# Pinning the instruction order across the seam of two output projections, and squaring a row in its own buffer

## The chip, the cores and the metric

The kernel runs on one core of a Trainium2 chip. The metric is device time in microseconds (us) of one execution. In the text PE is the matrix engine (TensorE), DVE is VectorE, ACT is ScalarE, POOL is GpSimd and SP is SyncE; POOL and SP mostly issue DMAs here.

## The reference

One transformer-like layer over a sequence of 1024 positions with width 1024, in float32. What matters here is the end of its first sub-layer and the start of the second:

```python
merged = sigmoid(gate_a) * a_out + sigmoid(gate_b) * b_out   # (1024, 1024)
x  = x + gt1 * (merged @ w_o)                                # output projection, residual
h2 = rmsnorm(x, norm2_g) * (1.0 + sc2) + sh2                 # needs sum(x*x) over the width
f_gate, f_up = split(h2 @ w_ffn_in)                          # 2 x 2816 wide
x  = x + gt2 * ((silu(f_gate) * f_up) @ w_ffn_out)
```

The root-mean-square norm needs, for each position, the sum of the squares of all 1024 values of the new `x`. So no row of `h2` can be made before the last block of the output projection is finished.

## The kernel before

**Layout.** Everything is kept transposed: 128 channels on the partitions, positions along the free dimension. The sequence is worked in two halves of 512 positions (`hf` 0 and 1). The output projection is a loop over `hf` and, inside it, over eight blocks `d` of 128 output channels (line 1330 and after). Each product is made of float32r matmuls in three passes: both operands are split in a high part and a rest, and `mm3` issues high x high, high x low, low x high. One block `d` is 8 x 3 = 24 matmuls into one PSUM bank; four such banks (`mm`) rotate.

**What one block d does.** I write d0 to d7 for the blocks of half 0 and d0' to d7' for those of half 1.

- `unit(w_o[d+1])` prepares the next weight block, one step ahead: SP loads it into one of three `raw` buffers, ACT copies it to a high part `wh`, DVE subtracts for the rest `wl`. Each of `wh` and `wl` has three buffers.
- `store(xk, x_rows(hf, d))`, despite its name a load issued on POOL's queue, brings 128x512 of the residual `x` into `xk`, one of two buffers of the tag `xs`.
- after the 24 matmuls, DVE forms the new row block `x1` from the bank, the gate `gt1` and `xk` (one scalar_tensor_tensor, called STT below). In half 0, `x1` lies in a `tmp()` buffer: tag `t2`, shown as `t` in the profile, four buffers.
- `sumsq` squares `x1` on ACT, for d > 0 into another `tmp()` buffer, and DVE adds it to the running sum `ss`. For d = 0 the square goes straight to `ss`. There is one `ss` buffer, so half 1's cannot be written before half 0's has been read.
- `store(x1d, x1)` writes the row block to DRAM, again on POOL's queue.
- in half 0 only: `m_split(m1, d-1)` splits a row of half 1's merged input (ACT cast, DVE subtraction), `m_load(m1, 1, d)` loads the next such row into one of two `hs` buffers, and for d = 1 to 6 `ada_next` does one 128x1024 dot product of the adaLN modulation on DVE (`mid<-mid,silu_c`, then a small `mod<-acc_mod,cc`). d7 splits both of the last two rows, 6 and 7; row 7 is loaded right before, when row 5's split has freed a buffer.
- in half 1 only: at d1', before its matmuls, `col_rstd(sums[0])` turns `ss` of half 0 into column sums with eight small matmuls (`at<-ones,ss`), DVE scales them (`ms`), POOL takes the power -1/2 (`rcol`), and before the matmuls of d2' `spread` broadcasts it over a bank (`at<-ident,rcol`). From then on `mod2` normalises half 0's rows. At d2' and d4', `first_unit` loads and splits the 128x1024 weight blocks `w_gate[4]` and `w_gate[5]` ahead of time into long-lived buffers (`j<-raw`).

**What sets the order.** A planner orders each engine's instructions at build time, by its own cost model and by which inputs it takes to be ready; program order is only a priority. The engines then run that order strictly. While the flag `in_order[0]` is true, each instruction issued through the wrapper is pinned behind the instruction traced just before it on the same engine:

```python
def call(*args, **kw):
    ins = f(*args, **kw)              # line 76, the line of nearly all instructions
    if in_order[0]:
        tc.keep_in_program_order(ins)
    return ins
```

This holds for PE, DVE, ACT and POOL arithmetic. DMAs issued on SP by `load` are always pinned; DMAs issued on POOL by `store` never are. In the projection loop the flag is set once in each pass by `in_order[0] = hf == 1 and d > 5` (line 1356), behind the line that issues `unit(w_o[d+1])`, so the weight preparation of a pass still runs under the flag of the pass before.

Of the kernel before, what the change touches and what calls it, by code (L numbers as in the profile page):

```python
# [38 lines left out]
def kernel(  # L39
# [24 lines left out]
    in_order = [False]  # L64
# [35 lines left out]
    def nm(s):  # L100
        n_names[0] += 1
        return f"{s}_{n_names[0]}"

    def mm_bank():
        return psum.tile([P, 512], F32, tag="mm", name=nm("mm"))
# [4 lines left out]
    def tmp(dt=F32):  # L110
        return t2.tile([P, 512], dt, tag="t2", name=nm("t2"))

    def stream(tag):
        return t2.tile([P, 512], F32, tag=tag, name=nm(tag), bufs=2)

    def midt(dt, shape):
        return mid.tile([P, 2048], dt, tag="mid", name=nm("mid")).rearrange(
            "p (a b) -> p a b", a=shape
        )

    def hid():
        return hpool.tile([P, 2048], F32R, tag="h", name=nm("h")).rearrange(
            "p (a b) -> p a b", a=4
        )
# [3 lines left out]
    def jt(dt, shape):  # L128
        return jpools[0].tile([P, 2048], dt, tag="j", name=nm("j")).rearrange(
            "p (a b) -> p a b", a=shape  # L130
        )
# [4 lines left out]
    def load(dst, src):  # L136
        tc.keep_in_program_order(nc.sync.dma_start(dst, src))

    def store(dst, src):
        nc.gpsimd.dma_start(dst, src)  # L140
# [10 lines left out]
    def raw_unit(src):  # L151
        r = wpool.tile([P, UNIT], F32, tag="raw", name=nm("raw"))
        load(r, src)
        return r

    def unit(src, eng=None, raw=None):
        r = raw if raw is not None else raw_unit(src)
        h = wpool.tile([P, UNIT], F32R, tag="wh", name=nm("wh"))
        l = wpool.tile([P, UNIT], F32R, tag="wl", name=nm("wl"))
        A.copy(h, r)  # L160
        (eng or V).tensor_tensor(l, r, h.bitcast(F32), op=ALU.subtract)
        return h, l

    def mm3(out, a, b, first, last):
        T.matmul(out, a[0], b[0], start=first, stop=False)
        T.matmul(out, a[0], b[1], start=False, stop=False)
        T.matmul(out, a[1], b[0], start=False, stop=last)
# [120 lines left out]
    def col_rstd(ss, n, r):  # L288

        pt = at_bank()  # L290
        for i in range(n):
            T.matmul(pt[:, i : i + 1], ss[:, i * P : (i + 1) * P], ones[:, 0:1], start=True, stop=True)
        rstd(pt[:, :n], n, r)

    def spread(r, n):

        bc = at_bank()
        for i in range(n):
            T.matmul(bc[:, i * P : (i + 1) * P], r[:, i : i + 1].to_broadcast([P, P]), ident,
                     start=True, stop=True)  # L300
        return bc[:, : n * P]

    def ss_tile():
        return small.tile([P, 640], F32, tag="ss", name=nm("ss"), bufs=1)

    rcol = [const.tile([P, 5], F32, tag=f"rcol{i}", name=f"rcol{i}") for i in range(4)]

    def sumsq(src, first, ss):
        if first:
            A.activation(ss, src, AF.Square)  # L310
        else:
            q = tmp()
            A.activation(q, src, AF.Square)
            V.tensor_tensor(ss, ss, q, op=ALU.add)

    def modulate(src, rb, k, sc, sh, hH, hL, dst):

        shift = mod[:, sh + k : sh + k + 1]
        V.scalar_tensor_tensor(out=dst, in0=src, scalar=mod[:, sc + k : sc + k + 1], in1=rb,
                               op0=ALU.mult, op1=ALU.mult)  # L320
        A.activation(hH, dst, AF.Identity, bias=shift)
        V.scalar_tensor_tensor(out=hL, in0=dst, scalar=shift, in1=hH.bitcast(F32),
                               op0=ALU.add, op1=ALU.subtract)
# [162 lines left out]
    def first_unit(i):  # L486

        r = raw_unit(w_gate[EARLY - 2 + i])
        h, l = (firsts[p][:, i * UNIT : (i + 1) * UNIT] for p in range(2))
        A.copy(h, r)  # L490
        V.tensor_tensor(l, r, h.bitcast(F32), op=ALU.subtract)
        return h, l
# [22 lines left out]
    def ada_next(more=True):  # L515
        if not ada_ahead:
            return
        col, gain, r = ada_ahead.pop(0)
        ada_dot(r, col)
        ada_end(col, gain)  # L520
        if more:
            ada_load()
# [11 lines left out]
    def ada_pair_load():  # L534
        i = ada_queue[0][0] - GT1
        t = midt(F32, 2)
        store(t, w_ada2[i : i + 2].rearrange("a p b -> p a b"))
        for j in range(2):
            col, gain = ada_queue.pop(0)
            ada_ahead.append((col, gain, t[:, j, :]))  # L540
# [15 lines left out]
    def x_rows(hf, k):  # L556
        return xT[k * P : (k + 1) * P, hf * HALF : (hf + 1) * HALF]

    def flat(t):
        return t.rearrange("p a b -> p (a b)")  # L560
# [665 lines left out]
    def m_tiles(kind):  # L1226
        return [(kind(F32R, 4), kind(F32R, 4)) for _ in range(2)]
# [3 lines left out]
    def m_load(m, hf, k, t=None):  # L1231
        m_src[k] = t = stream("hs") if t is None else t
        store(t, md[hf][k])

    def m_split(m, k):
        h, l = (x[:, k % 4, :] for x in m[k // 4])
        split(m_src.pop(k), h, l)
# [92 lines left out]
    for hf in range(2):  # L1330
        if hf == 1:
            h2[0] = [[hid(), hid()], [hid(), hid()]]
            x1B.extend([midt(F32, 4), midt(F32, 4)])
            h2m.extend([midt(F32, 4), midt(F32, 4)])
            for part in range(2):
                firsts[part] = flat(jt(F32R, 4))
        ss = ss_tile()[:, :HALF]

        def mod2(d):
            xk = stream("hs")  # L1340
            load(xk, x1d[d * P : (d + 1) * P, :HALF])
            hi, lo = (t[d // 4][:, d % 4, :] for t in h2[0])
            modulate(xk, rb, d, SC2, SH2, hi, lo, h2m[d // 4][:, d % 4, :])

        for d in range(KT):
            wo = wo_next
            if d < KT - 1:
                wo_next = unit(w_o[d + 1])
            elif hf == 0:
                wo_next = unit(w_o[0])  # L1350
            else:
                raw1 = raw_unit(w_gate[1])
                raw2.append(raw_unit(w_gate[2]))
            if hf == 1 and d == 6:
                early.append(unit(w_gate[0], V))
            in_order[0] = hf == 1 and d > 5
            if hf == 1 and d in (2, 4):
                early.append(first_unit(d // 2 - 1))
            xk = stream("xs")
            store(xk, x_rows(hf, d))  # L1360
            pw = mm_bank()
            for k in range(KT):
                if hf == 1 and (d, k) == (1, 0):
                    col_rstd(sums[0], NT, rcol[2])
                if hf == 1 and (d, k) == (2, 0):
                    rb = spread(rcol[2], NT)
                kc = slice(k * P, (k + 1) * P)
                mm3(pw, (wo[0][:, kc], wo[1][:, kc]),
                    (m[k // 4][0][:, k % 4, :], m[k // 4][1][:, k % 4, :]), k == 0, k == KT - 1)
            if hf == 1:  # L1370
                for i in {2: (0,), 3: (1,), 4: (2, 3), 5: (4,), 6: (5, 6), 7: (7,)}.get(d, ()):
                    mod2(i)
            x1 = tmp() if hf == 0 else x1B[d // 4][:, d % 4, :]
            V.scalar_tensor_tensor(out=x1, in0=pw, scalar=mod[:, GT1 + d : GT1 + d + 1], in1=xk,
                                   op0=ALU.mult, op1=ALU.add)
            sumsq(x1, d == 0, ss)
            store(x1d[d * P : (d + 1) * P, hf * HALF : (hf + 1) * HALF], x1)
            if hf == 0:
                if d == 0:
                    m1 = m_tiles(jt)  # L1380
                else:
                    m_split(m1, d - 1)
                m_load(m1, 1, d)
                if d == KT - 1:
                    m_split(m1, d)
                if d in (0, 2, 4):
                    ada_pair_load()
                if 0 < d < 7:
                    ada_next(False)
            if hf == 1 and d == KT - 1:  # L1390
                early.append(unit(None, V, raw1))
        in_order[0] = False
        sums.append(ss)
        if hf == 0:
            m = m1
# [319 lines left out]
    with tc.manual_schedule():  # L1715
# [172 lines left out]
        for n, (i, e) in enumerate(work):  # L1888
            _, _, b, first = OUT[i]
# [90 lines left out]
```

## Time and profile before

| | |
|---|---|
| median of 3 runs | 1253.28 us (1250.98 to 1254.64) |
| the profiled execution, its own time | 1254.18 us |
| its span (first to last instruction) | 1252.4 us |
| mean granted clock of PE | 0.997 |
| PE busy | 1222.5 us, 98% |
| DVE busy | 915.0 us, 73% |
| ACT busy | 578.7 us, 46% |
| first projection, last matmul of d7 begins | 558.81 us |
| second projection, last matmul of d0' begins | 564.25 us |

All instructions of the wrapper have one line, L76, so the profile is read by tiles and by time. Times within it count from the span's start. In the timeline a row gives the start, the duration, the engine, the operation, output<-inputs and, in brackets, the idle time before it with what ended it. The waits list who waited for whom: total, times and longest. The rows by stretch of time give the busy time of each engine, the granted clock of PE, the share of the DMA engines and the bandwidth.

### The profile page before, as it was taken

How to read it: one execution, taken by the hardware profiler on the slowest of the kernel's cores; microseconds unless marked ns; L12 is line 12 of the kernel's file. 1: busy time of each engine (PE TensorE's matmuls, PEld its weight loads, DVE VectorE, ACT ScalarE, POOL GpSimd, SP SyncE). 2: the span in 40 equal slices, each digit the busy share in tenths (PEclk: the TensorE clock that was granted, in tenths of full speed). 3: DMA queues.
4: the chain of work that ended last, by engine and by line, in shares of the span. 5: the costliest groups of instructions: out<-in, count | busy, mean ns of one | idle time of the engine just before them, and what ended most of it. 6: DMA issues, size and time to landing. Idle time of an engine off the chain costs nothing.

```text
span 1252.4 us, 15649 instructions
## 1 busy us (share of the span) xinstructions
PE 1222.5 (98%) x5634; PEld 1011.4 (81%) x5634; DVE 915.0 (73%) x1548; ACT 578.7 (46%) x938; POOL 184.6 (15%) x234
## 2 busy tenths in 40 slices
PE   5999999999999999998999999999999999999998
PEld 4888888888887888787888887888888887888887
DVE  8997884487897798965798756676766666565746
ACT  5477864367876333443454333333333334433342
POOL 1223430023342010322100000001010000010001
PEclk9999999999999999998999999999999999999999
DMA  9731258421157466886502444454555559896542
GB/s 362 272 101 60 76 188 296 143 97 51 60 176 234 154 219 226 277 275 226 207 34 101 168 168 164 156 212 182 194 196 180 180 185 374 318 353 230 198 156 101
DMA packets 77665, 236.29 MB, mean 189 GB/s; under 512 B 9362, under 2 KB 9362, under 8 KB 71571
## 3 DMA queue, kind: packets, MB, share of 16 engines
q1 hardware_dynamic: 55298, 142.48, 32.9%
q0 software_dynamic: 18832, 86.52, 19.5%
q10 hardware_dynamic: 3456, 6.29, 1.3%
q8 instruction: 44, 0.72, 0.2%
q14 instruction: 35, 0.28, 0.1%
HBM read 177.58 MB, written 57.67 MB: 188 GB/s over the span
## 4 chain that ended last, share of the span: by engine, by line
PE 63%; DVE 11%; DMA 11%; issue 9%; ACT 5%; POOL 1%; SPq 0%; ACTq 0%; DVEq 0%; POOLq 0%
PE at L76 34%; PE mm L76 29%; DVE mid L76 3%; DVE wl L76 3%; ACT wh L76 2%; DMA raw<-in_w_out_dram 1%; DMA raw<-in_w_ga_dram 1%; DMA hs<-in_w_ada_dram 1%; DVE hs L76 1%; DMA mid<-in_w_ada_dram 1%; DMA xs<-in_w_ada_dram 1%; DVE t L76 1%; ACT lb L76 1%; DVE raw L76 1%; DMA hs<-in_xT_dram 1%
## 5 line engine op out<-in xcount | busy, mean ns | idle before, releaser
L76 ACT CAST wh<-raw 128x1024 fp32r<-128x1024 f32 x155 | 162.5, 1051 | 158.5 <-PE mm L76 59.4
L76 DVE TENSOR_TENSOR wl<-raw,wh 128x1024 fp32r<-128x1024 f32 x141 | 171.9, 1220 | 68.2 <-ACT wh L76 67.0
L76 PE MATMUL mm<-mid,wh 128*128 128x512 f32 x696 | 215.2, 390 | 1.7 <-ACT mid L76 0.8
L76 PEld LDWEIGHTS mm<-mid,wh 128*128 128x128 f32 x696 | 130.3, 188 | 30.2 <-ACT mid L76 1.3
L76 PE MATMUL at<-j,wh 128*128 128x512 f32 x464 | 143.1, 389 | 0.0
L76 PE MATMUL mm<-mid,wl 128*128 128x512 f32 x348 | 135.4, 389 | 0.5 <-POOL wl L76 0.5
L76 PE MATMUL mm<-wh,h 128*128 128x512 f32 x384 | 128.8, 397 | 2.6 <-ACT h L76 2.6
L76 PEld LDWEIGHTS at<-j,wh 128*128 128x128 f32 x464 | 87.0, 188 | 18.6 <-ACT wh L76 0.4
L76 DVE TENSOR_TENSOR wl<-ws,wh 128x1024 fp32r<-128x1024 f32 (+1 forms) x55 | 62.0, 1127 | 44.0 <-ACT wh L76 44.0
L76 PE MATMUL mm<-j,wh 128*128 128x512 f32 x288 | 91.1, 398 | 0.2 <-ACT wh L76 0.2
L76 PE MATMUL at<-j,wl 128*128 128x512 f32 x232 | 90.4, 390 | 0.5 <-DVE wl L76 0.5
L76 PE MATMUL at<-h,wh 128*128 128x512 f32 x288 | 89.0, 390 | 0.0
L76 PEld LDWEIGHTS mm<-wh,h 128*128 128x128 f32 x384 | 71.2, 188 | 17.6 <-ACT h L76 3.9
L76 PE MATMUL mm<-h,wh 128*128 128x512 f32 x272 | 84.6, 392 | 0.0
L76 ACT CAST wh<-ws 128x1024 fp32r<-128x1024 f32 (+1 forms) x55 | 53.6, 974 | 58.8 <-DVE ws L76 42.4
L76 PEld LDWEIGHTS mm<-mid,wl 128*128 128x128 f32 x348 | 65.3, 188 | 14.5 <-POOL wl L76 1.0
L76 PE MATMUL mm<-wl,h 128*128 128x512 f32 x192 | 75.2, 392 | 0.3 <-DVE wl L76 0.3
L76 PEld LDWEIGHTS mm<-j,wh 128*128 128x128 f32 x288 | 55.2, 193 | 12.0 <-ACT wh L76 0.6
L76 PEld LDWEIGHTS at<-h,wh 128*128 128x128 f32 x288 | 53.9, 188 | 11.4 <-DVE mid L76 0.3
L76 PEld LDWEIGHTS mm<-h,wh 128*128 128x128 f32 x272 | 50.6, 188 | 10.4
L76 ACT ACTIVATE xs<-xs 128x512 f32<-128x512 f32 x21 | 13.3, 633 | 96.9 <-DVE xs L76 96.9
L76 PE MATMUL mm<-j,wl 128*128 128x512 f32 x144 | 57.1, 397 | 0.5 <-DVE wl L76 0.5
(282 smaller groups left out, 2559.2 us busy)
## 6 DMA issues: line engine op xcount, KB each, us to landing
raw<-in_w_gate_dram SPq DMA_DIRECT2D x28, 512.0 KB, 5.2
tA<-hid POOLq DMA_DIRECT2D x11, 1024.0 KB, 4.9
tB<-hid POOLq DMA_DIRECT2D x11, 1024.0 KB, 5.0
wo<-in_w_out_dram POOLq DMA_DIRECT2D x22, 512.0 KB, 6.1
wS<-wo POOLq DMA_DIRECT2D x11, 1024.0 KB, 5.4
raw<-wS SPq DMA_DIRECT2D x44, 256.0 KB, 3.2
raw<-tB SPq DMA_DIRECT2D x44, 256.0 KB, 4.0
raw<-in_w_out_dram SPq DMA_DIRECT2D x33, 256.0 KB, 5.1
```

Of the source, the lines that this page charges most:

```text
L76: ins = f(*args, **kw)
```

## The change

`in_order` becomes true for d6 and d7 of half 0 and for d0' and d1' of half 1 (d6' and d7' were pinned before). The two `first_unit` calls at d2' and d4' are pinned, too, each behind what was traced before it. With the rule of the wrapper that makes these fixed sequences:

- DVE: STT d6, add d6, rest of m1 row 5, adaLN dot and its end, `wl` of half 1's `w_o[0]`, STT d7, add d7, rests of m1 rows 6 and 7; later `wl` of `w_o[1]`, STT d0', `wl` of `w_o[2]`, `ms`, STT d1', add d1', `wl` of `w_o[3]`, `j` of `w_gate[4]`.
- ACT: square d6, cast of m1 row 5, `wh` of `w_o[0]`, square d7, casts of rows 6 and 7; later `wh` of `w_o[1]`, square d0', `wh` of `w_o[2]`, square d1', `wh` of `w_o[3]`, `j` of `w_gate[4]`.

In half 0, the square of a row block is written into `xk`, the `xs` buffer of the residual row that has just been used, in place of a `tmp()` buffer. Nothing is added or removed in instructions or bytes.

```diff
-    def sumsq(src, first, ss):
+    def sumsq(src, first, ss, q=None):
         if first:
             A.activation(ss, src, AF.Square)
         else:
-            q = tmp()
+            q = tmp() if q is None else q
             A.activation(q, src, AF.Square)
             V.tensor_tensor(ss, ss, q, op=ALU.add)
...
             if hf == 1 and d == 6:
                 early.append(unit(w_gate[0], V))
-            in_order[0] = hf == 1 and d > 5
+            in_order[0] = d > 5 or hf == 1 and d < 2
             if hf == 1 and d in (2, 4):
+                in_order[0] = True
                 early.append(first_unit(d // 2 - 1))
+                in_order[0] = False
             xk = stream("xs")
             store(xk, x_rows(hf, d))
             pw = mm_bank()
...
-            sumsq(x1, d == 0, ss)
+            sumsq(x1, d == 0, ss, xk if hf == 0 else None)
```

## The prediction, made before the changed kernel was run

> **What bounds the kernel now.** I read the page first, then the waits of PE over the whole span and over 490 to 620 us, then busy time by short stretches, then the timelines of PE, ACT, DVE and POOL around the seam of the two projections.
>
> ```profile
> span 1252.4 us, 15649 instructions
> PE 1222.5 (98%) x5634; PEld 1011.4 (81%) x5634; DVE 915.0 (73%) x1548; ACT 578.7 (46%) x938; POOL 184.6 (15%) x234
> PEclk9999999999999999998999999999999999999999
> PE at L76 <- DVE ss L76: 11.4, 2, 8.1
> PE at L76 <- DVE ss L76: 3.3, 1, 3.3
> 565.00:570.00 5.00, 2.06 (x10) 1.97 (x11) 3.02 (x5) 3.02 (x4) 0.83 (x2) 0.84 0.90 295
> 570.00:575.00 5.00, 5.00 (x14) 3.84 (x13) 0.77 (x1) 0.10 (x1) 2.24 (x2) 0.50 0.62 226
> ```
>
> PE is the bound: 98% busy, so time is won only where PE waits or runs slowly. The fourth row (whole span) has an 8.1 us wait near the start; the fifth (490 to 620 us) has one of 3.3 us for `ss`, the sum of squares, which the change aims at. It costs more than 3.3 us: the last two rows give the granted clock in their third column from the end. It is 0.50 in 570 to 575 us, the only dent in the page's row of clocks. The matmuls on both sides of the wait, and of the same step at the next seam, price it:
>
> ```profile
> 558.81 0.39 PE L76 MATMUL mm<-mid,wl 128*128 128x512 f32 x1
> 559.03 0.61 PE L76 MATMUL mm<-j,wh 128*128 128x512 f32 x2
> 559.49 0.39 PE L76 MATMUL mm<-j,wl 128*128 128x512 f32 x1
> 564.25 0.39 PE L76 MATMUL mm<-j,wl 128*128 128x512 f32 x1
> 567.94 1.50 PE L76 MATMUL at<-ones,ss 128*128 128x1 f32 x8 [3.30 <-DVE ss L76]
> 569.29 1.20 PE L76 MATMUL mm<-j,wh 128*128 128x512 f32 x2
> 577.36 0.39 PE L76 MATMUL mm<-j,wl 128*128 128x512 f32 x1
> 616.37 0.40 PE L76 MATMUL at<-h,wl 128*128 128x512 f32 x1
> 617.41 0.70 PE L76 MATMUL at<-h,wh 128*128 128x512 f32 x2
> ```
>
> Block d0' ran undisturbed: from last start to last start 564.25 - 558.81 = 5.44 us for 24 matmuls, of which 559.03 - 558.81 = 0.22 lie ahead of its first, so a block takes 5.22 from first to last start. The same column sums at the other seam (between the last two rows) hold the next block up by 617.41 - 616.37 = 1.04 us; here it was 569.29 - 564.25 = 5.04, so 4.00 too many. Block d1' took 577.36 - 569.29 = 8.07 instead of 5.22, so 2.85 too many, at the halved clock. Together **6.85 us**, 0.55% of the time, is what a perfect repair is worth.
>
> Why `ss` was late is on ACT and DVE:
>
> ```profile
> 564.98 1.04 ACT L76 CAST j<-raw 128x1024 fp32r<-128x1024 f32 x1 [4.92 <-DMA raw<-in_w_gate_dram]
> 565.93 0.62 ACT L76 ACTIVATE t<-t 128x512 f32<-128x512 f32 x1
> 561.59 0.75 DVE L76 SCALAR_TENSOR_TENSOR t<-mm,mod,xs 128x512 f32<-128x512 f32 x1 [2.80 <-DMA x1d<-t]
> 566.06 1.23 DVE L76 TENSOR_TENSOR j<-raw,j 128x1024 fp32r<-128x1024 f32 x1 [2.58 <-ACT j L76]
> 567.20 0.68 DVE L76 TENSOR_TENSOR ss<-ss,t 128x512 f32<-128x512 f32 x1
> ```
>
> STT d7 ended at 562.34. Its square started at 565.93, because the planner had put the cast of a gate weight (`j<-raw`, of `first_unit`) ahead of it and that weight's DMA was late. The last add had the `j` subtraction ahead of it in the same way.
>
> **The change part by part.**
>
> *Pinning first_unit and d7.* Both `j` instructions now come behind half 1's d1', so square and add of d7 follow STT d7 directly. No instruction is added; the `j` work (1.04 on ACT, 1.23 on DVE) moves to d2', where a 5.4 us block has room for it. Worth up to 6.85 us. What is late next depends on STT d7 and on what the new order puts ahead of it, so the steps of d6 need prices.
>
> *Pinning d6 and d7.* The weight block of d0' (`wl` of `w_o[0]`) now stands on DVE behind STT d6, add d6, the rest of row 5 and a dot product. PE reaches it at 559.03 and needs `wl` in its third matmul, at 559.49. The prices are start to start:
>
> ```profile
> 541.44 0.69 DVE L76 TENSOR_TENSOR ss<-ss,t 128x512 f32<-128x512 f32 x1 [0.52 <-ACT t L76]
> 542.05 0.68 DVE L76 TENSOR_TENSOR j<-hs,j 128x512 fp32r<-128x512 f32 x1
> 542.65 0.20 DVE L76 TENSOR_SCALAR mod<-acc_mod,cc 128x1 f32<-128x1 f32 x1
> 547.64 1.21 DVE L76 SCALAR_TENSOR_TENSOR mid<-mid,silu_c 128x1024 f32<-128x1024 f32 x1
> 548.78 0.74 DVE L76 SCALAR_TENSOR_TENSOR t<-mm,mod,xs 128x512 f32<-128x512 f32 x1
> 549.45 0.20 DVE L76 TENSOR_SCALAR mod<-acc_mod,cc 128x1 f32<-128x1 f32 x1
> 549.57 1.21 DVE L76 TENSOR_TENSOR wl<-raw,wh 128x1024 fp32r<-128x1024 f32 x1
> 550.70 0.68 DVE L76 TENSOR_TENSOR ss<-ss,t 128x512 f32<-128x512 f32 x1
> 553.48 0.74 DVE L76 SCALAR_TENSOR_TENSOR t<-mm,mod,xs 128x512 f32<-128x512 f32 x1
> 554.31 0.64 ACT L76 ACTIVATE t<-t 128x512 f32<-128x512 f32 x1 [0.52 <-ACT wh L76]
> 555.27 0.68 DVE L76 TENSOR_TENSOR ss<-ss,t 128x512 f32<-128x512 f32 x1
> 556.31 0.75 DVE L76 SCALAR_TENSOR_TENSOR t<-mm,mod,xs 128x512 f32<-128x512 f32 x1 [0.35 <-PE mm L76]
> ```
>
> STT to square 0.83 (553.48, 554.31), square to add 0.96 (555.27), add to rest 0.61 (541.44, 542.05), rest 0.60, dot 1.14 (547.64, 548.78), its end 0.12 (549.45, 549.57), and `wl` itself 1.21: 5.47 us. Called T6, the start of STT d6 must thus lie before 559.49 - 5.47 = 554.02, or PE waits for the difference. Here it was 556.31. In the kernel before this costs nothing, since `wl` did not stand behind it. The ACT side fits: the cast of `wh` (1.04) would end near T6 + 3, before 559.03.
>
> *Squares in the row buffers.* This sets T6. A `xs` buffer is free for row d+2 only after the add, not after the STT: by 550.70 + 0.68 - (548.78 + 0.74) = 1.86 us for d4. In return `x1` no longer shares four `t2` buffers with squares. The row of d6 landed like this:
>
> ```profile
> 550.36 0.54 POOL L140 DMA_DIRECT2D xs<-in_xT_dram  x1
> xs<-in_xT_dram POOLq DMA_DIRECT2D x1, 256.0 KB, 5.8
> DMA to landing us min/median/max: 2.8/5.1/10.1
> ```
>
> The second row is the DMA view of the moment of the first, the last is from the view of the `xs` tile. 550.36 + 5.8 = 556.16, and STT d6 began 0.15 later: it waited for its row. The label names PE, but block d6 had its last matmul start one block before d7's, at 558.81 - 5.44 = 553.37, long before. STT d7 is labelled with the store `x1d<-t`, but it may also have waited for its row; the change shortens the first wait and lengthens the second.
>
> When does add d4 end in the new kernel? If the planner kept its order to the letter, at 551.38; then the row is issued at 551.4, lands at 557.2, T6 is 557.4 and PE waits 3.4. But pinning moves the rest of row 5 (0.60) and the dot product of d6 (547.64, 1.14) from ahead of STT d4 to behind add d6. Add d4 then ends 1.74 earlier, at 549.64; the row is issued at 549.7, lands at 555.5, T6 = 555.65 and PE waits 1.6. At best the row is early, and T6 is the end of block d6, about 553.8: no wait. I take 1.6, which stands on the moved rows, and keep 0 and 3.4. The rule that speaks against the change is strict order itself: the Trainium skill ("TensorE: Matmul & The Clock Gate", Architectural detail) calls ACT and DVE strict FIFO, and the square behind the `j` cast shows it. On the row's landing the skill's "DMA: Bandwidth & Descriptors" (Anatomy of one DMA) gives a fit of 2.0 us plus bytes over 436 GB/s, by my estimate 2.6 us for 256 KB; the measured 5.8 disagrees and decides. By the fit T6 would be 553.8 and the wait nothing.
>
> *m1's row 7.* Its load now waits for the rest of row 5, at T6 + 3.1 = 558.75; with the median 5.1 of the `xs` rows of the same size it lands at 563.9, and cast and rest (about 0.6 and 0.7, as the square and the rest above) make it ready at 565.2. PE needs it at matmul 23 of 24, at 559.03 + 1.6 + 22 x 5.44/24 = 565.6. Covered by 0.4 us; with the 5.8 of above it would cost 0.3, with 10.1 it would cost 4.6. I put it at nothing.
>
> *d0' and d1'.* `ms` now stands behind square d0', `wh` and `wl` of `w_o[2]`.
>
> ```profile
> 569.72 1.95 POOL L76 TENSOR_TENSOR rcol<-ms,nhalf 128x4 f32<-128x4 f32 x1 [0.33 <-DVE ms L76]
> 617.84 1.04 POOL L76 TENSOR_TENSOR rcol<-ms,nhalf 128x4 f32<-128x4 f32 x1 [4.42 <-DVE ms L76]
> PE mm L76 <- ACT xs L76: 0.4, 1, 0.4
> PE at L76 <- DVE wl L76: 0.7, 1, 0.7
> ```
>
> After d0' ends, column sums about 0.8 (1.04 less one matmul's step), square 0.64, cast 1.04, `wl` 1.21, `ms` as small as the adaLN end, 0.20, and the power, 1.04 or 1.95, make 4.9 to 5.8 us. PE meanwhile has the sums and d1', 0.8 + 5.44 = 6.2, before `spread` needs the result. I take nothing, with a cover of 0.4 to 1.3; if `w_o[2]` comes later than that, each us is lost.
>
> Sum: -6.85 + 1.6 = **-5.2 us**: 1254.18 to 1249.0 in a profiled execution. That execution was 0.90 above the median, so the median goes from 1253.28 to **1248.1**. The shift carries to the end: the last two rows above are PE's longest waits in 620 to 1000 us and from there to the end, 0.4 and 0.7, so nothing there can swallow it.
>
> **The rivals.**
>
> *Full gain (0.15).* The row of d6 lands in time, at the 2.8 us minimum of its tile. No wait at d0': -6.85, 1246.4. Against it: 5.8 at this very place.
>
> *The stall only moves (0.20).* DVE keeps its lag, T6 is 557.4, and PE waits 3.4 us for `wl`. A wait of 3.30 was followed by the half clock here, costing 2.85: -6.85 + 3.4 + 2.85 = -0.6, 1252.7. By the skill's clock page (The HAM clock gate) the clock falls after an idle window of about 3.4 us; two matmuls in the middle could then save it, and this case would give 1249.8. The trace's 3.30 is just under that figure and fell, so I keep 1252.7.
>
> *Slower (0.13).* The row of d6 lands as the latest of its tile did, after 10.1 us: issued at 549.7, T6 is 559.95, and PE waits 5.9 us plus 2.85 for the clock. Row 7 of m1 follows at T6 + 3.1 and, late by the same congestion, adds about 2 us. -6.85 + 5.9 + 2.85 + 2 = +3.9: 1257.2. The point from which it decides is a wait of 4.0 at the half clock, T6 = 558.0. For it: the tile's own maximum. Against: the row at this very place took 5.8.
>
> *It doesn't do what it says (0.05).* Pinning binds only to the instruction traced before; an unpinned cast can still slide ahead of square d7. No change, 1253.3.
>
> **How the numbers follow.** The forecast of 1248.1 has 0.47. Faster and slower count from 0.3%, 3.8 us, about what a measurement of this kernel can tell from no change (the three runs span 3.66). Faster: forecast 0.47, full gain 0.15 and 0.03 of the moved stall, 0.65. Same: 0.17 and 0.05, 0.22. Slower 0.13. Range: from the full gain less a run's scatter, 1245.5, to the moved and missing effects plus scatter, 1254.5. The forecast's own range is 1246.4 to 1249.9.
>
> **What would show it.** Right: no `ss` wait at PE's `at<-ones,ss`, granted clock 1.00 throughout, d1' lasting 5.2 us; one PE wait for `wl` or `m1` of 0 to 3.4 us at d0'; square d7 within 1 us of STT d7. Wrong: a wait over 3.3 us at d0' with a new dent in the clock, STT d6 after 557, or `spread` waiting for `rcol`.

## The result, and the profile after

| | before | after |
|---|---|---|
| median of 12 runs each, taken side by side | 1253.98 us (1249.39 to 1258.49) | 1249.72 us (1247.15 to 1250.57) |
| ratio after / before, 95% interval | | 0.9964 (0.995 to 0.9978) |
| the profiled execution, its own time | 1254.18 us | 1249.81 us |
| mean granted clock of PE in it | 0.997 | 1.000 |

The change is worth 0.36% of the time, 4.5 us by the ratio (2.8 to 6.3), against 5.2 forecast. The median 1249.72 lies within the range on record.

First the head of the page of the kernel after, then its waits of PE over 490 to 620 us, then two stretches of busy time (the columns are those of the rows shown before: length, PE, weight loads, DVE, ACT, POOL, granted clock, DMA share, GB/s).

```profile
span 1248.0 us, 15657 instructions
...
PE 1219.6 (98%) x5634; PEld 1008.8 (81%) x5634; DVE 915.1 (73%) x1548; ACT 577.8 (46%) x938; POOL 184.0 (15%) x234
...
PEclk9999999999999999999999999999999999999999
```

```profile
PE mm L76 <- ACT mid L76: 1.0, 2, 0.6
PE at L76 <- DVE mid L76: 1.0, 1, 1.0
PE mm L76 <- DVE mid L76: 0.4, 2, 0.2
```

```profile
565.00:570.00 5.00, 5.00 (x28) 4.25 (x27) 2.17 (x4) 1.57 (x2) 1.08 (x2) 1.00 0.81 284
570.00:575.00 5.00, 5.00 (x28) 4.27 (x27) 2.23 (x5) 1.58 (x3) 2.18 (x3) 1.00 0.64 197
```

The 8 in the row of clocks is gone, and so is the 3.3 us wait for `ss`; the waits that are left are for tiles shown as `mid`: one of 0.98 at 489.64, ahead of the projection, and four of 0.2 to 0.6 for the merged input at the start of it. In the stretch where PE had been at half clock it is busy all 5.00 us at 1.00. DVE is as busy as before: 915.0 us before and 915.1 after.

The matmuls of PE at the same places as before, in the kernel after:

```profile
560.61 0.62 PE L76 MATMUL mm<-j,wh 128*128 128x512 f32 x2
561.07 0.39 PE L76 MATMUL mm<-j,wl 128*128 128x512 f32 x1
...
565.83 0.40 PE L76 MATMUL mm<-j,wl 128*128 128x512 f32 x1
566.06 0.95 PE L76 MATMUL at<-ones,ss 128*128 128x1 f32 x8
566.87 0.70 PE L76 MATMUL mm<-j,wh 128*128 128x512 f32 x2
...
572.21 0.39 PE L76 MATMUL mm<-j,wl 128*128 128x512 f32 x1
572.44 0.38 PE L76 MATMUL at<-ident,rcol 128*128 128x128 f32 x2
```

From the last matmul of d0' to the first of d1' the column sums now cost 566.87 - 565.83 = 1.04 us where they cost 5.04, and d1' takes 572.21 - 566.87 = 5.34 where it took 8.07. I call the stretch from the first matmul of d0' to the last of d1' **the seam**: 577.36 - 559.03 = 18.33 before, 572.21 - 560.61 = 11.60 after. So 6.73 us came back there: 4.00 at the sums and 2.73 in d1', at the full clock.

The two profiled executions differ by 1254.18 - 1249.81 = 4.37 only. The missing 2.4 lie outside the seam: PE came to d0' at 560.61 and not at 559.03 (1.58), and the part from the second column sums to the end of the trace was 636.56 long and not 635.77 (0.8; I did not follow where). From the end of d1' to those second sums both kernels take 39.24. The section on the prediction shows where the 1.58 arose, and that the new order did not make it.

Next, the instructions of DVE, ACT and POOL that the prediction followed, from the timelines of the kernel after; the last two rows are from its DMA view and end with the time to landing of these two DMAs.

```profile
549.74 0.54 POOL L140 DMA_DIRECT2D xs<-in_xT_dram  x1 [1.19 <-DVE ss L76]
...
555.37 0.75 DVE L76 SCALAR_TENSOR_TENSOR t<-mm,mod,xs 128x512 f32<-128x512 f32 x1 [1.21 <-PE mm L76]
...
558.46 0.54 POOL L140 DMA_DIRECT2D hs<-md  x1
...
559.48 2.35 DVE L76 TENSOR_TENSOR wl<-raw,wh 128x1024 fp32r<-128x1024 f32 x2
561.75 0.74 DVE L76 SCALAR_TENSOR_TENSOR t<-mm,mod,xs 128x512 f32<-128x512 f32 x1
...
562.57 0.63 ACT L76 ACTIVATE xs<-t 128x512 f32<-128x512 f32 x1 [3.32 <-issue]
...
563.24 0.69 DVE L76 TENSOR_TENSOR ss<-ss,xs 128x512 f32<-128x512 f32 x1 [0.75 <-ACT xs L76]
...
569.85 0.15 DVE L76 TENSOR_SCALAR ms<-at 128x4 f32<-128x4 f32 x1
570.10 1.03 POOL L76 TENSOR_TENSOR rcol<-ms,nhalf 128x4 f32<-128x4 f32 x1 [1.71 <-DVE ms L76]
...
574.90 1.05 ACT L76 CAST j<-raw 128x1024 fp32r<-128x1024 f32 x1
...
xs<-in_xT_dram POOLq DMA_DIRECT2D x1, 256.0 KB, 5.3
hs<-md POOLq DMA_DIRECT2D x1, 256.0 KB, 3.3
```

The square of d7 begins 0.82 us after its STT (561.75, 562.57) where it was 4.34 behind. The running sum is complete at 563.24 + 0.69 = 563.93, and PE asks for it at 566.06. The `j` cast, which stood ahead of that square before, begins at 574.90, and the row has no wait at all.

The row of `wl` shows a count of 2: not only `w_o[0]` but also `w_o[1]` stands ahead of STT d7. The list given with the change has `w_o[1]` behind it; the list is wrong there. The loop clears the flag at the end of each half, so the weight preparation in the pass of d0' is traced unpinned, and the planner moved it forward. The same holds on ACT: both casts `wh` (557.26, 2.00 us together) stand ahead of the square of d7. STT d7 begins 0.98 us after the bank was complete (560.38 + 0.39, the last matmul of d7). With 566.06 - 563.93 = 2.1 us in hand at the sum this costs nothing.

### The profile page after: what moved, and what is told of

It reads as the page before. It is cut to its first block, busy times and chain, and to the rows that moved or that the text cites. A ratio compares the mean times of both kernels' runs of the same rounds, so it can differ in the third digit from the quotient of the medians.

```text
span 1248.0 us, 15657 instructions
## 1 busy us (share of the span) xinstructions
PE 1219.6 (98%) x5634; PEld 1008.8 (81%) x5634; DVE 915.1 (73%) x1548; ACT 577.8 (46%) x938; POOL 184.0 (15%) x234
## 4 chain that ended last, share of the span: by engine, by line
PE 63%; DVE 12%; issue 11%; DMA 9%; ACT 3%; POOL 1%; SPq 0%; ACTq 0%; POOLq 0%; DVEq 0%
PE at L76 32%; PE mm L76 31%; DVE mid L76 3%; DVE wl L76 3%; ACT wh L76 2%; DMA wS<-wo 2%; DMA raw<-in_w_out_dram 1%; DMA raw<-in_w_ga_dram 1%; DMA wo<-in_w_out_dram 1%; DVE hs L76 1%; DMA mid<-in_w_ada_dram 1%; DVE t L76 1%; DVE ws L76 1%; DVE raw L76 1%; DVE xs L76 1%
## 5 line engine op out<-in xcount | busy, mean ns | idle before, releaser
L76 DVE TENSOR_TENSOR ol<-raw,oh 128x1024 fp32r<-128x1024 f32 x30 | 36.5, 1223 | 27.8 <-ACT oh L76 27.3
```

## The experiments

The theory: the whole gain comes from the two `first_unit` calls. Their cast and subtraction wait for a late weight DMA at the head of ACT's and DVE's queues, with the small square and add behind them that PE needs. The main rivals: the gain comes from the fixed order of d6 and d7, or from the row buffers. And for the forecast's second term: a wait for `wl` is near, and costs what the prediction says.

### One part of the change at a time

**first_unit_only.** Of the change only the pins of the two `first_unit` calls.

```diff
-            in_order[0] = d > 5 or hf == 1 and d < 2
+            in_order[0] = hf == 1 and d > 5
...
-            sumsq(x1, d == 0, ss, xk if hf == 0 else None)
+            sumsq(x1, d == 0, ss)
```

> Only the two first_unit calls are pinned; squares stay in tmp buffers, d6 to d1' stay unpinned. My theory (the whole loss is the j cast and j subtraction standing ahead of square d7 and add d7): the ss wait at the column sums is gone, clock 1.00 throughout, 4 to 6 us faster than before, within 1.5 us of the full change. Rival A (the row buffers do it, by freeing t2 buffers for STT d7): STT d7 still late, ss wait of 1 us or more stays, gain under 2 us. Rival B (d6 and d7 must be pinned too): another unpinned instruction stands ahead of square d7, gain under 2 us.

Measured: 1248.75 against 1253.31 us, 0.9966 (0.9952 to 0.998). The seam is 11.60 us. ACT and PE in its timelines:

```profile
562.55 0.63 ACT L76 ACTIVATE t<-t 128x512 f32<-128x512 f32 x1 [1.66 <-DVE t L76]
...
565.30 0.95 PE L76 MATMUL at<-ones,ss 128*128 128x1 f32 x8
...
566.22 1.05 ACT L76 CAST j<-raw 128x1024 fp32r<-128x1024 f32 x1
```

With these pins alone the square of d7 stands ahead of the cast `j<-raw`, and the sums have no wait. The two pins bring all of it.

**rows_only.** No new pin; only the squares go to the row buffers.

```diff
-            in_order[0] = d > 5 or hf == 1 and d < 2
+            in_order[0] = hf == 1 and d > 5
             if hf == 1 and d in (2, 4):
-                in_order[0] = True
                 early.append(first_unit(d // 2 - 1))
-                in_order[0] = False
```

> Only the squares move to the row buffers; nothing new is pinned. My theory: the j cast still stands ahead of square d7, the ss wait of about 3 us and the halved clock stay, time as before within 2 us. Rival A: STT d7 and square d7 come earlier, the wait shrinks under 2 us, 3 us or more faster. The longer hold of a row buffer (about 1.9 us) could also make STT d6 and d7 later, and the time up to 1 us longer.

Measured: 1250.57 against 1253.31 us, 0.9989 (0.9973 to 1.0005): too close to 1 to be called a gain. The planner keeps the order of the kernel before at d7. The timelines of ACT and PE, and a stretch of busy time:

```profile
562.63 1.05 ACT L76 CAST j<-raw 128x1024 fp32r<-128x1024 f32 x1 [3.26 <-DMA raw<-in_w_gate_dram]
563.58 0.62 ACT L76 ACTIVATE xs<-t 128x512 f32<-128x512 f32 x1
...
565.59 1.05 PE L76 MATMUL at<-ones,ss 128*128 128x1 f32 x8 [1.64 <-DVE ss L76]
```

```profile
565.00:570.00 5.00, 4.41 (x16) 3.72 (x17) 2.50 (x4) 0.77 (x2) 3.48 (x4) 0.66 0.75 237
```

The square still waits behind the late cast. ACT waited 3.26 for its data here and not 4.92, and PE's wait is 1.64 and not 3.30. But the clock fell all the same, for 3.41 us by the trace's record of the clock, and the seam is 15.11. Whether the squares' place makes the cast less late, or this execution had an earlier DMA, one profile can't tell.

**pins_only** and **no_d67_pins.** All pins with the squares in `tmp()`; and the whole change without the pins of d6 and d7.

```diff
# pins_only
-            sumsq(x1, d == 0, ss, xk if hf == 0 else None)
+            sumsq(x1, d == 0, ss)
# no_d67_pins
-            in_order[0] = d > 5 or hf == 1 and d < 2
+            in_order[0] = hf == 1 and (d > 5 or d < 2)
```

> All pins of the change, squares still in tmp buffers. My theory: same as the full change within 1 us, 3.5 to 5.5 us faster than before; STT d6 starts at the end of block d6 or at its row's landing, whichever is later, and the row is issued about 1.8 us earlier than in the full change because its buffer is free after the STT. Rival A (row buffers needed): STT d7 waits for a t2 buffer until an x1d store has landed, ss late, gain under 2 us.

> The full change without the pins of d6 and d7 in half 0. My theory: no ss wait, 4 to 6.5 us faster than before; wl of w_o[0] no longer stands behind STT d6, so no wait for wl at d0' in any case: equal to the full change or up to 1 us better. Rival B (these pins carry the gain): the order ahead of square d7 is again bad, gain under 2 us.

Measured: 0.9967 (0.9954 to 0.9979) and 0.9965 (0.995 to 0.998), both with a seam of 11.60. Neither the row buffers nor the pins of d6 and d7 can be seen in the time; the intervals leave room for about 1.8 us either way.

**full_again** and **first_unit_again.** Both kernels once more, unedited and side by side, to see whether anything separates them.

> The full change once more, for a second execution. My theory: 3.5 to 5.5 us faster than before; no ss wait; at d0' either no wait for wl or one of up to 1 us, according to whether the row of d6 lands before or after block d6 ends. If PE again starts d0' at about 560.6 us, the 1.6 us lost ahead of d0 belong to the change; if at 559.0 or so, they were scatter.

> Only the two first_unit calls pinned, beside the full change on the same chip. My theory: equal to the full change within 1 us, as the other parts neither give nor take more than that.

Measured: 0.9967 (0.9954 to 0.9981) and 0.9965 (0.9951 to 0.9978); 1247.93 and 1248.03 us. The rest of the change gives or takes nothing that can be seen. In the profile of full_again PE came to d0' at 560.58, which its expectation had named as the sign that the late arrival belongs to the change; the section on the prediction says why I don't keep that.

### Is it the order, or the lateness of what stands ahead?

**j_resident.** The kernel before, its order on ACT and DVE held as it was. But the cast and subtraction of the first `first_unit` read a buffer that is long there (`silu_c`) in place of the arriving weight block. The weight is still loaded; the values of this one block are left out of the result. `after(x, y)` pins x behind y; what stands in angle brackets is told in words, and the lines that keep hold of these two instructions are left out.

```diff
         if i == 0:
+            r = silu_c
+            after(A.copy(h, r), <cast wh of w_o[2]>)
+            after(V.tensor_tensor(l, r, h, op=ALU.subtract), <rest wl of w_o[2]>)
+            return h, l
```

> The kernel before with its own order on ACT and DVE (the j cast and j subtraction of the first first_unit still stand ahead of square d7 and add d7), but these two read an array that is already on the chip instead of the gate weight that is just being loaded; the load itself is still issued. The values of one weight block are thus left out. Tells order from lateness. My theory (the late DMA at the head of a fixed queue is the loss, the order alone costs about 1 us on each engine and is covered): no ss wait or one under 0.5 us, 4 to 5.5 us faster than before. Rival (the order itself is the loss): ss wait of 1 us or more, gain under 2.5 us.

Measured: 1248.7 against 1253.1 us, 0.9962 (0.9948 to 0.9976), the seam 11.60. ACT and PE:

```profile
558.96 1.05 ACT L76 CAST j<-silu_c 128x1024 fp32r<-128x1024 f32 x1
559.92 0.63 ACT L76 ACTIVATE t<-t 128x512 f32<-128x512 f32 x1
...
563.48 0.95 PE L76 MATMUL at<-ones,ss 128*128 128x1 f32 x8
```

The cast still stands directly ahead of the square of d7, and the full gain is there. So the order alone costs nothing that can be seen: a cast of 1.05 us fits. What costs is that the cast waits for a DMA and holds the square with it.

### What a wait costs at this seam

**wl_late_4** and **wl_late_8** lengthen DVE's chain ahead of `wl` of `w_o[0]` in the changed kernel, by 4 and 8 instructions that leave `ss` as it is. **ss_late_5** and **ss_late_9** do the same ahead of the column sums, behind the last split of d7.

```diff
# wl_late_4 (8: range(8))
             elif hf == 0:
+                for _ in range(4):
+                    V.tensor_tensor(ss, ss, ss, op=ALU.max)
                 wo_next = unit(w_o[0])
# ss_late_5 (9: range(9))
                 if d == KT - 1:
                     m_split(m1, d)
+                    for _ in range(5):
+                        V.tensor_tensor(ss, ss, ss, op=ALU.max)
```

> The full change with four extra DVE instructions (ss = max(ss, ss), 0.6 us each, the result unchanged) pinned ahead of the wl of half 1's w_o[0]. Tests the step that wl stands behind STT d6 with next to no cover. My theory: in the profile of the full change wl ended about 0.4 us before PE used it, so PE now waits about 2.0 us for wl at d0' and the time is 2 to 3.7 us above the full change (the upper end if the clock falls for one period of 3.4 us). Rival (the cover is larger than the profile of one execution shows): no wait at d0', time unchanged within 1 us.

> The same with eight. My theory: PE waits about 4.4 us for wl at d0', the granted clock falls to 0.5 for at least one period of 3.4 us, time 6 to 8 us above the full change. Rival: the wait is under 2.5 us, time under 3 us above.

> The full change with five such DVE instructions behind the splits of d7, so that ss is late again without any late DMA; the planner puts three of them behind STT d0'. Tests the price of the wait itself. My theory: PE waits about 2.7 us at the column sums, the clock falls for one or two periods of 3.4 us, d1' takes 7 to 8 us instead of 5.3, time 4.4 to 5.6 us above the full change, about that of the kernel before. Rival (the clock does not fall below a wait of about 3.3 us): 2.7 us above.

> The same with nine, seven of them behind STT d0'. My theory: PE waits about 5.1 us at the column sums, the clock falls for two periods, time 7.5 to 9 us above the full change.

DVE and PE of wl_late_4 (the timelines), with two stretches of busy time:

```profile
554.40 0.75 DVE L76 SCALAR_TENSOR_TENSOR t<-mm,mod,xs 128x512 f32<-128x512 f32 x1 [1.49 <-DMA xs<-in_xT_dram]
...
558.50 2.86 DVE L76 TENSOR_TENSOR ss<-ss 128x512 f32<-128x512 f32 x4
561.28 1.22 DVE L76 TENSOR_TENSOR wl<-raw,wh 128x1024 fp32r<-128x1024 f32 x1
...
562.55 0.80 PE L76 MATMUL mm<-j,wl 128*128 128x512 f32 x1 [3.06 <-DVE wl L76]
```

```profile
560.00:565.00 5.00, 2.45 (x6) 1.97 (x7) 4.97 (x7) 1.66 (x3) 0.55 (x1) 0.67 0.28 84
565.00:570.00 5.00, 5.00 (x16) 3.95 (x15) 1.09 (x2) 0.00 (x0) 0.54 (x1) 0.64 0.80 267
```

PE of wl_late_8, of ss_late_5 and of ss_late_9, and the stretches of the last:

```profile
564.39 0.79 PE L76 MATMUL mm<-j,wl 128*128 128x512 f32 x1 [5.20 <-DVE wl L76]
```

```profile
558.44 0.61 PE L76 MATMUL mm<-j,wh 128*128 128x512 f32 x2
559.05 0.50 PE L76 MATMUL mm<-j,wl 128*128 128x512 f32 x1
...
567.53 1.68 PE L76 MATMUL at<-ones,ss 128*128 128x1 f32 x8 [3.16 <-DVE ss L76]
```

```profile
574.20 1.86 PE L76 MATMUL at<-ones,ss 128*128 128x1 f32 x8 [5.97 <-DVE ss L76]
```

```profile
570.00:575.00 5.00, 0.80 (x4) 0.80 (x4) 3.98 (x6) 0.00 (x0) 0.55 (x2) 0.62 0.39 134
575.00:580.00 5.00, 5.00 (x15) 4.13 (x16) 1.30 (x2) 1.56 (x2) 0.92 (x1) 0.50 0.04 4
580.00:585.00 5.00, 5.00 (x25) 4.22 (x24) 0.72 (x1) 0.00 (x0) 0.11 (x1) 0.85 0.44 153
```

All of them beside each other. The half-clock time is from the trace's record of the clock; the fourth column is the seam less the undisturbed 11.60; the last is the ratio's distance from 0.9965 (the change had 0.9964 and, in full_again, 0.9967), times 1253 us:

| kernel | PE's wait | half clock | seam lost | ratio (95%) | us by the ratio |
|---|---|---|---|---|---|
| rows_only | 1.64 | 3.41 | 3.51 | 0.9989 (0.9973 to 1.0005) | 3.0 |
| wl_late_4 | 3.06 | 6.83 | 6.17 | 0.9993 (0.9978 to 1.0009) | 3.5 |
| ss_late_5 | 3.16 | 6.83 | 6.95 | 1.0019 (1.0006 to 1.0033) | 6.8 |
| before | 3.30 | 6.83 | 6.73 | 1 | 4.4 |
| wl_late_8 | 5.20 | 6.83 | 8.03 | 1.0032 (1.0015 to 1.0049) | 8.4 |
| ss_late_9 | 5.97 | 10.24 | 9.63 | 1.0045 (1.0028 to 1.0062) | 10.0 |

The lost time of the seam is the wait and 1.9 to 3.8 us more, nearly all of it the price of the clock (in ss_late_5 0.3 of it lies in d0', which took 5.53 us from first to last start and not 5.21). In ss_late_5, wl_late_8 and ss_late_9 28 of the 30 runs had a mean granted clock of 0.997 or less, and there the ratio agrees with the seam of the profile. In wl_late_4 only the profiled run of ten had, and there, as in the kernel before, the typical run pays less than the profiled one: 1254.48 us in the profiled execution of wl_late_4, 1252.28 in the median.

The expectations had these too small: each wait came out 0.5 to 1.1 us longer. One added instruction took 0.7 us and not 0.6 ((561.28 - 558.50) / 4), and in wl_late_4 PE also came to d0' early. The price by the ratio lies 0.4 to 1.2 us above the expected range in wl_late_8, ss_late_5 and ss_late_9, and inside it in wl_late_4.

## Why the prediction was right, and where its terms were off

**The bound and the mechanism: right.** PE was the bound, the 3.30 us for `ss` were the repairable loss, and the cast and subtraction of `first_unit` were its cause. first_unit_only shows the cause (the pins of these alone give 0.9966) and j_resident shows the way it acts (same order, data there, 0.9962).

**A perfect repair, -6.85: right for the profiled execution, too large for the typical one.** The seam gave back 6.73, as 11.60 in every kernel without a wait shows. The 0.12 is d1' itself, 5.34 undisturbed where the prediction took 5.22. But the profiled execution had 6.83 us at half clock in it, and not every execution has: half of 6.83 us is 0.27% of the time, so a run with a mean granted clock of 0.998 or more can't have lost that much. Of 91 runs of the kernel before, beside the kernels of the experiments, 37 had a mean granted clock of 0.997 or less and a median of 1254.29 us; the other 54 were above and had 1251.79. The profile, at 0.997 and 1254.18, was one of the 37. Among the runs of the kernels with a seam of 11.60 none was at 0.997 or below; those measured beside these 91 runs had medians of 1247.9 to 1248.8, so that the 37 lose about 6 us against them and the 54 about 3.5. The prediction took off the execution's distance from the median, 0.90, at the end, on both sides of the sum, as though the loss itself were the same in every run. The typical loss is what the change gains, 4.5.

**The wait for `wl`, +1.6: didn't come in the change, and was a few tenths where it did.** Of the chain that led to it, the first links held: the row of d6 was issued at 549.74 (forecast 549.7) and landed after 5.3 us (forecast 5.8), at 555.04. STT d6 began at 555.37 (forecast 555.65). What was off is the other end: PE came to d0' at 560.61, not at 559.03. In the row above the STT is released by PE, whose block d6 ended then, and not by the DMA. From there `wl` was ready at 559.48 + 1.21 = 560.69, 0.4 us ahead of the matmul at 561.07.

Had PE come early, the wait would still not have been 1.6. In wl_late_4 PE came at 558.88, and STT d6 did wait for its row (1.49), as forecast. The added instructions put `wl` off by 561.28 - 558.50 = 2.78; the wait of 3.06 is 0.28 more, so that the change by itself would have waited about 0.3 in that execution. In ss_late_5 PE came at 558.44, and its third matmul began 0.61 after that, at 559.05, where it is 0.46 without a wait (561.07 - 560.61): a wait of 0.15. The sum had three terms a little too long: in these two executions PE came to d0' 9.9 us after the issue of the row (559.03 - 549.7 = 9.3 in the forecast), STT d6 began 5.2 to 5.4 us after it (5.95), and from there to the end of `wl` it was 5.3 (5.47).

PE's late arrival was not made by the new order. It came to d0' at 558.04 to 562.62 over the thirteen profiles of this study; the six with the order of the full change up to there have 558.44, 558.58, 558.88, 560.58, 560.61 and 562.62. Most of the 1.58 arose at two waits for the merged input that the kernel before did not have there; between 520.11 and 522.01 PE's lag behind the kernel before goes from 0.29 to 1.51:

```profile
520.95 0.50 PE L76 MATMUL mm<-mid,wh 128*128 128x512 f32 x1 [0.45 <-ACT mid L76]
521.67 0.50 PE L76 MATMUL mm<-mid,wh 128*128 128x512 f32 x1 [0.22 <-DVE mid L76]
```

The instructions of PE, DVE, ACT, POOL and SP follow in the same order in both kernels until after 528 us, so these waits lie ahead of anything that the change reorders. full_again had both (0.35 and 0.23), wl_late_8 neither. The kernels that leave out the pins of d6 and d7 or the row buffers (first_unit_only, no_d67_pins, pins_only) are not faster than the whole, so the typical price is nothing that the runs can tell. The estimate of 2.6 us for such a row from the Trainium skill ("DMA: Bandwidth & Descriptors", Anatomy of one DMA) was off here, too, where 5.3 was measured.

The two errors nearly cancel: -6.85 + 1.6 = -5.2 was forecast, -4.5 + 0 came. The mechanism was right; that the sum came within 0.7 us of the result is in part luck.

**The covered steps: right.** Row 7 of the merged input was issued at 558.46 and landed after 3.3 us (forecast 558.75 and 5.1); PE didn't wait for it. `rcol` was done at 570.10 + 1.03 = 571.13 and `spread` came at 572.44: a cover of 1.3, the upper end of the 0.4 to 1.3.

**The rivals.** *Full gain* (1246.4) is the mechanism that the profile of the change shows: no wait at d0'. But the row took 5.3 us and not 2.8; `wl` was in time because PE came late. Its time was too low because the typical loss was 4.5. *The stall only moves* (1252.7) is what wl_late_4 made on purpose: a wait of 3.06 for `wl` with the half clock, 0.9993. Its mechanism and price are real; only the wait is not there in the change. *Slower* had its point of decision at a wait of 4.0. By the table it lies lower, near 3.1 (wl_late_4 0.9993, ss_late_5 1.0019), because the gain to be lost was 4.5 and not 6.85. *It doesn't do what it says* came true at one place: the unpinned cast and subtraction of `w_o[1]` did slide ahead of the square and the STT of d7. Their data was there, and it costs nothing.

**The clock.** The Trainium skill ("TensorE: Matmul & The Clock Gate", The HAM clock gate) puts the fall behind an idle window of about 3.4 us. The periods in the traces are indeed multiples of 3.41 us, but one period followed a wait of only 1.64 us, and in ss_late_9 (last section) one followed a wait of 0.89; the measurement decides, and the prediction was right to keep the price of the clock at a wait below the page's figure.

## What to carry to other kernels

Look for a prefetch that waits for a DMA ahead of the small instructions which the bound engine needs next; in a queue that runs in order, it is the lateness of the first that costs, so hold the prefetch behind them, and one or two pins do it without fixing the rest. Price a wait of the matrix engine with the half-clock time that follows it: at this seam 3 us of waiting cost 6 to 7. Before a loss is taken from one profiled execution, see from the mean granted clock of the other runs whether all of them have it.

## What the runs showed of the hardware that was not expected

A wait of 1.64 us, followed by 0.9 us of one-column matmuls, halved the clock for 3.41 us; 0.95 us of those matmuls without a wait did not. Waits of 3.06 to 5.20 were followed by 6.83 us and one of 5.97 by 10.24. The length of a wait alone does not decide. The profile of ss_late_9 has one more half-clock period of 3.41 us, from 516.63 on, at the start of the projection, where nothing had been added:

```profile
516.43 1.52 PE L76 MATMUL mm<-mid,wh 128*128 128x512 f32 x2 [0.89 <-ACT mid L76]
515.00:520.00 5.00, 4.02 (x10) 2.55 (x10) 3.47 (x5) 1.62 (x3) 1.80 (x3) 0.66 0.94 321
```

Waits of 0.29 and 0.23 us stand just ahead of it, at 514.09 and 514.81. In wl_late_4 a wait of 1.18 us at 512.78 and one of 0.22 right behind it left the clock at 1.00. What else decides was not tried.

The same 256 KB, issued on POOL's queue 8.7 us apart in one execution, landed after 5.3 and 3.3 us. A deadline that is met by 0.4 us, as `wl` met its own here, is met by luck.
